# Splitting projection weights further ahead, on other engines, with extra transposes at the start of a two-layer hybrid encoder

## The chip, the cores and the metric

The kernel is one program on one core of a Trainium2 chip. The metric is the device time of one execution in microseconds. The kernel before was timed three times: 1618.01, 1619.09 and 1620.23 us, a median of 1619.09 us.

## The reference

The model is an encoder trunk of two layers over one sequence of 512 tokens and 1024 features. Each layer normalises its input, projects it with a matrix of 1024 x 4608, mixes over the sequence with two groups of heads, projects back, and adds a mixture of 16 experts, each of which picks 64 tokens.

```python
IN_WIDTHS = [RET_WIDTH] * 4 + [HGRN_WIDTH] * 5        # nine groups of 512 columns

def hybrid_mixer(xn, w_in, ret_g, hgrn_g, w_out, lb):
    proj = xn @ w_in
    rq, rk, rv, rg, hq, hf_fwd, hf_bwd, hi, hg = jnp.split(proj, splits, axis=-1)
    q, k = rotary(rq), rotary(rk) * RET_HEAD_DIM ** -0.5
    r_out = retention, forward and backward, of (q, k, rv), normalised, * silu(rg)
    q2, v2 = silu(hq) * HGRN_HEAD_DIM ** -0.5, hi
    f = lb + (1 - lb) * sigmoid(hf)                   # one per direction
    h_out = gated scan, forward and backward, of (q2, 1 - f, v2, log f), normalised, * silu(hg)
    return jnp.concatenate([r_out, h_out], axis=-1) @ w_out

h = x
for layer in range(2):
    h = h + hybrid_mixer(rms_norm(h, norm1_g[layer]), w_in[layer], ...)
    h = h + expert_choice_ffn(rms_norm(h, norm2_g[layer]), ...)
return rms_norm(h, final_norm_g)
```

Everything is float32.

## The kernel before

The instructions of every engine stand in the order in which the Python code issues them; the framework adds the semaphore waits. Each engine works through its own queue in order, so an instruction that waits holds up all that stand behind it on its engine.

**Start.** `start` (L364) loads nothing itself: the input rows come in four DMAs, one for each tile of 128 tokens. `turn_in` (L345) transposes blocks of 128 x 128 on TensorE into PSUM tiles `pb`, for the feature blocks 0 to 3 and one token tile after another. `stream` (L353) scales each feature block and splits it into a high part (ScalarE, L362) and a low part (VectorE, L363). `norm_gain` (L211) transposes one small tile of gains.

**Projections.** A float32 product is made of three products of rounded parts: high weight times high input, low weight times high input, high weight times low input. `proj` (L458) makes one group of 512 columns of the input projection: four quarters of 256 input features, each of 24 matmuls of 512 columns (L479). The nine groups are taken in the order `GROUPS`, counted here from 0 (`n`) or as first to ninth: silu query, the two forget gates (second and third), the value `v2` (fourth), then the rotary query and key, the retention value and gate, and the last gate.

**Splitting.** `split` (L437) makes the parts of the weights, one quarter at a time. The high part is a copy on ScalarE (L450), the low part a subtraction (L453) on VectorE, or on GpSimd for odd quarters of the groups 7 and 2, which are the fourth and the seventh in order. `proj` calls `split` at the start of each quarter with a number of quarters to be ahead: one in the first three groups and in the ninth, two in the others. Each split quarter occupies one of 22 slots of SBUF from its splitting until the last of its 24 matmuls; the raw half group that feeds two quarters occupies another one. Slots are handed out in order, and `pump` issues a weight load on SyncE's queue when a slot is free.

**Scans.** With the fourth group the scan over the first pair of the gated heads begins (`hgrn_pair`, L575). It is a generator that is advanced between blocks of six matmuls, with a budget for each group. Its first steps are, for both heads of the pair: the sum of the two keys on GpSimd (L604), the product of gates and query on VectorE (L605), two interleaved products (L615, L616), a high part on ScalarE (L618), a low part on VectorE (L621), then a product with a 0/1 matrix on TensorE (L629, four matmuls for each head). Six levels follow, each with products on VectorE (L587, L592), a product of decays on GpSimd (L597), a copy on ScalarE (L567) and score matmuls (L642). The second pair of heads goes through the same steps during the fifth and sixth group. In a layer the evacuation of a projection is on VectorE (L489) and ScalarE (L510, L511).

**Experts.** After the mixer come the output projection (L963), the routing and 16 experts in eight pairs, whose weights (192 MB in a layer) pass once through the same slots.

Of the kernel before, what the change touches and what calls it, by code (L numbers as in the profile page):

```python
# [16 lines left out]
P = 128  # L17
S = 512
D = 1024
NT = S // P  # L20
# [45 lines left out]
class Kernel:  # L66
# [298 lines left out]
    def start(self):  # L365

        self.begin(0)
        self.new_squares()
        for tt in range(NT - 1):
            self.squares(tt, 0, 0, 512, self.nc.scalar)  # L370
            self.squares(tt, 1, 512, 512, self.nc.vector)
        self.turn_in(range(4), range(2))
        self.norm_gain()
        self.turn_in(range(4), range(2, NT))
        self.stream(0)
        self.split(0)
        self.stream(1)
# [57 lines left out]
    def split(self, upto):  # L435


        nc = self.nc
        while self.nsplit <= min(upto, 4 * len(self.GROUPS) - 1):
            i = self.nsplit  # L440
            self.nsplit += 1
            g, j, jj = self.GROUPS[i // 4], i % 4 // 2, i % 2
            if jj == 0:
                self.raw = self.take(("in", self.mix_layer, g, j))
            part = self.slot([2, 2, 512], F32R)
            wh, low = part[:, 0], part[:, 1]
            src = self.raw.rearrange("p a k c -> p (a k) c")[:, 2 * jj:2 * jj + 2]
            e = nc.gpsimd if self.GROUPS[i // 4] in (7, 2) and i % 2 or i == 0 and self.mix_layer else nc.vector
            for ks in ((slice(0, 1), slice(1, 2)) if i == self.mix_layer == 0 else (slice(0, 2),)):
                nc.scalar.activation(wh[:, ks], src[:, ks], AF.Copy)  # L450
                if ks.start:
                    e = nc.gpsimd
                e.tensor_tensor(low[:, ks], src[:, ks], wh[:, ks], op=OP.subtract)  # L453
            self.parts[i] = part
            if jj:
                self.put(self.raw)

    def proj(self, n, natural, evacuate):  # L458


        nc = self.nc
        pg = [self.pj() for _ in range(4)]
        for q in range(4):
            self.split(4 * n + q + (2 if 2 < n < 8 else 1))
            part = self.parts.pop(4 * n + q)
            wh, low = part[:, 0], part[:, 1]

            if n == q == 0:
                order = [(c, k2, m) for k2 in range(2) for m in (0, 2, 1) for c in range(4)]
            elif n == 0 and q < 3:  # L470
                order = [(c, k2, m) for k2 in range(2) for c in range(4) for m in range(3)]
            else:
                order = [(c, k2, m) for c in range(4) for k2 in range(2) for m in range(3)]
            for i, (c, k2, m) in enumerate(order):
                cs = slice(c * P, (c + 1) * P)
                k = 2 * q + k2
                w, x = (wh, low, wh)[m][:, k2], (self.xH, self.xH, self.xL)[m][k // 4][:, k % 4]
                lhsT, rhs = (x[:, cs], w) if natural else (w[:, cs], x)
                nc.tensor.matmul(pg[c], lhsT=lhsT, rhs=rhs, start=(k == 0 and m == 0), stop=(k == ND - 1 and m == 2))  # L479
                if k == ND - 1 and m == 2:  # L480
                    evacuate(c, pg[c])
                if i == 23:
                    self.put(part)
                if i % 6 == 5:
                    yield
# [961 lines left out]
```

## Time and profile before

| what | value |
|---|---|
| median of three runs | 1619.09 us |
| the profiled execution | 1617.86 us |
| its span, first to last instruction | 1616.1 us |
| TensorE busy | 1537.6 us, 95% |
| VectorE, ScalarE, GpSimd busy | 671.3, 479.2, 207.8 us |
| matmuls of the input projection (L479) | 424.9 us, 1728 instructions |
| matmuls of the expert gates (L1208) | 476.7 us, 2048 instructions |
| read from HBM | 459.03 MB |

The profiled execution takes 1617.86 us, 1.76 us more than its span, since some time passes outside the first and last instruction. In the rows below, PE is TensorE, PEld its weight loads, DVE VectorE, ACT ScalarE, POOL GpSimd and SP SyncE. A row of a timeline merges neighbouring instructions of one line; the text in brackets is idle time of the engine before the row, with what ended it. In a table of stretches the column PEclk is the granted TensorE clock as a share of full speed. Layer 0 begins its fourth group at about 84 us, layer 1 at about 879 us.

### The profile page before, as it was taken

Reading aid. Unit: us, or ns where it says so; the run is one execution under the profiler, and the core shown is the slowest. Engines: PE = TensorE matmul, PEld = TensorE weight load, DVE = VectorE, ACT = ScalarE, POOL = GpSimd, SP = SyncE. Lnnn points to the kernel's source line nnn. Section 1 sums busy time; section 2 is a strip of 40 time slices with the busy share of each in tenths; the row PEclk is TensorE's granted clock in tenths of the full one; section 3 lists DMA queues with packets and bytes.
Section 4 is the critical chain, followed back from the end, with each engine's and each line's share of the span. In section 5 each row is a group of like instructions: output and inputs, shape, how many; then the busy total and the mean of one; then the engine's idle time right before and its main releaser. Section 6 shows DMA issues by size and latency. Waiting matters only on the chain. (4 is left out here: it accounts for less than half of the span.)

```text
span 1616.1 us, 20044 instructions
## 1 busy us (share of the span) xinstructions
PE 1537.6 (95%) x8020; PEld 957.6 (59%) x8020; DVE 671.3 (42%) x1132; ACT 479.2 (30%) x888; POOL 207.8 (13%) x197
## 2 busy tenths in 40 slices
PE   8999999989999999999999999999899999999986
PEld 6878787765354534533488787877545345444333
DVE  4488855661021312311255988375502123222113
ACT  4444444542221200200243444355313102112003
POOL 1043431100000000011001234320000000000201
PEclk9999999999999999999999999999999999999999
DMA  7211122679999999999960211217899999999997
GB/s 262 80 53 53 67 85 79 235 287 357 426 421 426 426 426 427 426 426 427 401 232 27 79 53 53 100 65 274 327 395 426 424 426 426 427 426 427 427 425 267
DMA packets 94605, 464.53 MB, mean 287 GB/s; under 512 B 7904, under 2 KB 16288, under 8 KB 48432
## 3 DMA queue, kind: packets, MB, share of 16 engines
q1 hardware_dynamic: 93040, 458.35, 69.9%
q0 software_dynamic: 1472, 4.90, 0.8%
q8 instruction: 63, 1.03, 0.2%
q14 instruction: 30, 0.25, 0.0%
HBM read 459.03 MB, written 4.19 MB: 287 GB/s over the span
## 5 line engine op out<-in xcount | busy, mean ns | idle before, releaser
L1208 PE MATMUL pj<-s,s 128*64 128x512 f32 x2048 | 476.7, 596 | 18.1 <-DMA s<-in_w_up_dram 14.6
L479 PE MATMUL pj<-s,s 128*128 128x512 f32 x1728 | 424.9, 400 | 3.5 <-DVE s L551 1.6
L479 PEld LDWEIGHTS pj<-s,s 128*128 128x128 f32 x1728 | 323.2, 191 | 70.8 <-DVE s L551 2.5
L1208 PEld LDWEIGHTS pj<-s,s 128*64 128x64 f32 x2048 | 172.2, 137 | 279.9 <-issue 206.9
L1352 PE MATMUL pb<-s,t 128*64 128x512 f32 x896 | 197.6, 594 | 5.6 <-ACT t L1246 2.7
L1352 PEld LDWEIGHTS pb<-s,t 128*64 128x64 f32 x896 | 64.0, 137 | 128.9 <-issue 115.0
L1256 DVE SCALAR_TENSOR_TENSOR t<-pb,sm,t 128x512 fp32r<-128x512 f32 (+1 forms) x34 | 24.4, 719 | 240.6 <-ACT t L1255 239.2
L1268 DVE TENSOR_TENSOR s<-s,pb 128x512 f32<-128x512 f32 (+1 forms) x112 | 67.3, 662 | 130.1 <-PE pb L1263 130.1
L1125 POOL TENSOR_TENSOR t<-s,t 128x512 fp32r<-128x512 f32 x16 | 20.9, 1330 | 696.8 <-ACT t L1123 696.8
L453 DVE TENSOR_TENSOR s<-s,s 128x1024 fp32r<-128x1024 f32 (+1 forms) x63 | 81.4, 1303 | 47.5 <-ACT s L450 47.3
L963 PE MATMUL pj<-s,s 128*128 128x512 f32 x384 | 95.1, 398 | 0.4 <-DVE t L489 0.4
L1173 DVE COPY sm<-pb 128x2 f32<-128x2 f32 x16 | 2.5, 159 | 203.2 <-PE pb L1170 203.2
L1255 ACT ACTIVATE t<-pb,sm 128x512 fp32r<-128x512 f32 (+1 forms) x34 | 22.5, 662 | 194.8 <-PE pb L1352 183.3
L963 PEld LDWEIGHTS pj<-s,s 128*128 128x128 f32 x384 | 69.9, 189 | 16.0 <-DVE t L489 1.3
L1184 ACT ACTIVATE t<-pb 128x512 fp32r<-128x512 f32 x16 | 9.6, 602 | 221.8 <-PE pb L1182 221.8
L450 ACT ACTIVATE s<-s 128x1024 fp32r<-128x1024 f32 (+1 forms) x73 | 74.1, 1035 | 0.1
L1151 PEld LDWEIGHTS pb<-t,t 128*128 128x128 f32 x512 | 65.7, 202 | 14.2 <-issue 9.7
L1151 PE MATMUL pb<-t,t 128*128 128x256 f32 x512 | 70.2, 295 | 2.1 <-DVE t L1135 1.3
L1263 PE MATMUL pb<-t,t 128*128 128x512 f32 (+1 forms) x256 | 66.7, 401 | 0.1
L1263 PEld LDWEIGHTS pb<-t,t 128*128 128x128 f32 x256 | 44.7, 188 | 33.1 <-issue 19.4
L1229 ACT ACTIVATE t<-pj,sm 128x512 f32<-128x512 f32 x32 | 22.0, 687 | 139.4 <-PE pj L1208 139.4
L567 ACT ACTIVATE s<-s 128x256 f32<-128x256 f32 x96 | 35.2, 415 | 80.1 <-DVE s L587 74.6
(235 smaller groups left out, 1587.2 us busy)
## 6 DMA issues: line engine op xcount, KB each, us to landing
s<-in_w_gate_dram SPq DMA_DIRECT2D x124, 1024.0 KB, 19.5
s<-in_w_up_dram SPq DMA_DIRECT2D x124, 1024.0 KB, 19.5
s<-in_w_down_dram SPq DMA_DIRECT2D x112, 1024.0 KB, 19.5
s<-in_w_in_dram SPq DMA_DIRECT2D x34, 1024.0 KB, 4.9
s<-in_w_down_dram SPq DMA_DIRECT2D x32, 512.0 KB, 10.4
s<-in_w_out_dram SPq DMA_DIRECT2D x8, 1024.0 KB, 4.8
s<-in_x_dram SPq DMA_DIRECT2D x8, 512.0 KB, 3.7
s<-in_w_gate_dram SPq DMA_DIRECT2D x8, 512.0 KB, 11.3
```

Of the source, the lines that this page charges most:

```text
L450: nc.scalar.activation(wh[:, ks], src[:, ks], AF.Copy)
L453: e.tensor_tensor(low[:, ks], src[:, ks], wh[:, ks], op=OP.subtract)
L479: nc.tensor.matmul(pg[c], lhsT=lhsT, rhs=rhs, start=(k == 0 and m == 0), stop=(k == ND - 1 and m == 2))
L567: self.nc.scalar.activation(kv[:, :, e], src, AF.Copy)
L963: nc.tensor.matmul(po[tt, f], lhsT=x, rhs=w, start=(k == 0 and i == 0), stop=(k == ND - 1 and i == 2))
L1151: nc.tensor.matmul(pt[:, i], lhsT=x[:, tt, k % 2::2], rhs=oh[:, tt], start=(tt == 0 and x is self.picked[u][0]), stop=(tt == NT - 1 and x ...
L1208: nc.tensor.matmul(pg[n + 2 * f][e * CAP:(e + 1) * CAP], lhsT=self.xe[:, k, at + e * CAP:at + (e + 1) * CAP], rhs=w[e][:, f * 512:(f + 1) ...
L1255: nc.scalar.activation(yH[0][:, cs], py, AF.Copy, scale=gate)
L1256: v.scalar_tensor_tensor(yL[0][:, cs], py, gate, yH[0][:, cs], op0=OP.mult, op1=OP.subtract)
L1263: nc.tensor.matmul(pc, lhsT=ohT[:, tt * P:(tt + 1) * P], rhs=y[:, cs], start=(y is yH[0]), stop=(y is yL[0]))
L1268: v.tensor_tensor(dst, dst, pc, op=OP.add)
L1352: nc.tensor.matmul(py[f][e * CAP:(e + 1) * CAP], lhsT=hT[:, k, e * CAP:(e + 1) * CAP], rhs=W[e][:, k2, f * 512:(f + 1) * 512], start=(k == ...
```

## The change

Three things are edited. At the start of layer 0, 16 transposes of the identity into a PSUM tile that nobody reads stand between the transposes of the input: five after the first token tile, and two, two and seven after the others. The odd quarters of the fourth group have their low part made on VectorE. The number of quarters that splitting is ahead comes from `lead_of`: in the first group one for the first two quarters and two for the last two (before: one), in the second group two (before: one), in the third group three and then four (before: one), and the rest as before.

```diff
-        self.turn_in(range(4), range(2))
-        self.norm_gain()
-        self.turn_in(range(4), range(2, NT))
+        unread = self.pj()
+        for tt, n in enumerate((5, 2, 2, 7)):
+            self.turn_in(range(4), [tt])
+            if tt == 1:
+                self.norm_gain()
+            for _ in range(n):
+                self.nc.tensor.transpose(unread[:, :P], self.ident, self.ident)
...
-            e = nc.gpsimd if self.GROUPS[i // 4] in (7, 2) and i % 2 or i == 0 and self.mix_layer else nc.vector
+            e = nc.gpsimd if self.GROUPS[i // 4] == 2 and i % 2 or i == 0 and self.mix_layer else nc.vector
...
+    @staticmethod
+    def lead_of(n, q):
+        if n == 2:
+            return 3 if q < 2 else 4
+        return 1 if n == 8 or n == 0 and q < 2 else 2
...
-            self.split(4 * n + q + (2 if 2 < n < 8 else 1))
+            self.split(4 * n + q + self.lead_of(n, q))
```

In the changed kernel the lines behind the first edit stand 5 lower, and those behind `lead_of` 12 lower: the low part L453 is L458, the evacuation L489 is L501, L604 is L616, L597 is L609, L605 is L617, L615 and L616 are L627 and L628, L621 is L633, L329 stays.

TensorE at the start of the program, from the last transpose of the first token tile on, before (`s_1` and `s_2` are the input, the four `pb` the PSUM tiles of its transposes, L214 the small transpose of the gains):

```order
L350 MATMUL pb_117<-ident,s_1_78 128x128
L350 MATMUL pb_114<-ident,s_1_78 128x128
L350 MATMUL pb_115<-ident,s_1_78 128x128
L350 MATMUL pb_116<-ident,s_1_78 128x128
L350 MATMUL pb_117<-ident,s_1_78 128x128
L214 MATMUL pj_126<-ident,t_3_83 128x16
L350 MATMUL pb_114<-ident,s_2_79 128x128
```

The same place now (`pj_114` is the unread tile):

```order
L350 MATMUL pb_118<-ident,s_1_78 128x128
L379 MATMUL pj_114<-ident 128x128 x5
L350 MATMUL pb_115<-ident,s_1_78 128x128
L350 MATMUL pb_116<-ident,s_1_78 128x128
L350 MATMUL pb_117<-ident,s_1_78 128x128
L350 MATMUL pb_118<-ident,s_1_78 128x128
L214 MATMUL pj_132<-ident,t_3_83 128x16
L379 MATMUL pj_114<-ident 128x128 x2
L350 MATMUL pb_115<-ident,s_2_79 128x128
```

The unread transposes stand in TensorE's own queue, so the transposes of the next token tile begin after them.

VectorE in the first group of layer 0, around the four short instructions that make the row norms (L329 to L332), before:

```order
L326 SCALAR_TENSOR_TENSOR sm_250<-sm_101 128x4
L453 TENSOR_TENSOR s_40_253<-s_6_99,s_40_253 128x1024
L329 RECIPROCAL sm_250<-sm_250 128x4
L330 TENSOR_TENSOR sm_250<-sm_250 128x4
L331 SCALAR_TENSOR_TENSOR sm_250<-sm_250 128x4
L332 SCALAR_TENSOR_TENSOR sm_249<-sm_250 128x4
L453 TENSOR_TENSOR s_46_299<-s_27_162,s_46_299 128x1024
```

The same place now:

```order
L326 SCALAR_TENSOR_TENSOR sm_267<-sm_101 128x4
L458 TENSOR_TENSOR s_41_270<-s_6_99,s_41_270 128x1024
L458 TENSOR_TENSOR s_42_273<-s_28_179,s_42_273 128x1024
L329 RECIPROCAL sm_267<-sm_267 128x4
L330 TENSOR_TENSOR sm_267<-sm_267 128x4
L331 SCALAR_TENSOR_TENSOR sm_267<-sm_267 128x4
L332 SCALAR_TENSOR_TENSOR sm_266<-sm_267 128x4
L458 TENSOR_TENSOR s_49_321<-s_28_179,s_49_321 128x1024
```

The low part of the second group's first quarter has moved ahead of the reciprocal, and the second quarter's low part stands where the first one stood.

VectorE from the third to the fourth group of layer 0, from the low parts of the third group's stretch to the first low part of the scan, before (`pj` rows are the evacuation of the third group):

```order
L453 TENSOR_TENSOR s_79_611<-s_70_494,s_79_611 128x1024
L489 TENSOR_TENSOR s_57_390<-pj_524,s_42_289 128x512
L489 TENSOR_TENSOR s_57_390<-pj_525,s_42_289 128x512
L489 TENSOR_TENSOR s_58_391<-pj_526,s_42_289 128x512
L489 TENSOR_TENSOR s_58_391<-pj_527,s_42_289 128x512
L453 TENSOR_TENSOR s_86_660<-s_77_564,s_86_660 128x1024
L605 TENSOR_TENSOR s_88_671<-s_57_390,s_47_308 128x1024 x2
L615 TENSOR_TENSOR s_89_672<-s_89_672,s_47_308 128x256x2
L616 TENSOR_TENSOR s_89_672<-s_59_392,s_88_671 128x256x2
```

The same place now:

```order
L458 TENSOR_TENSOR s_82_609<-s_71_484,s_82_609 128x1024
L458 TENSOR_TENSOR s_83_612<-s_79_560,s_83_612 128x1024
L458 TENSOR_TENSOR s_85_641<-s_79_560,s_85_641 128x1024
L501 TENSOR_TENSOR s_59_410<-pj_544,s_45_311 128x512
L501 TENSOR_TENSOR s_59_410<-pj_545,s_45_311 128x512
L501 TENSOR_TENSOR s_60_411<-pj_546,s_45_311 128x512
L501 TENSOR_TENSOR s_60_411<-pj_547,s_45_311 128x512
L617 TENSOR_TENSOR s_90_691<-s_59_410,s_50_330 128x1024 x2
L627 TENSOR_TENSOR s_91_692<-s_91_692,s_50_330 128x256x2
```

All four low parts of the fourth group now stand ahead of the evacuation of the third, and none is left between the evacuation and the first step of the scan.

GpSimd at the same place before, from the first low part of the fourth group on (`s_92_700` is the second one):

```order
L453 TENSOR_TENSOR s_85_657<-s_70_494,s_85_657 128x1024
L604 TENSOR_TENSOR s_89_672<-s_59_392 128x512
L604 TENSOR_TENSOR s_90_681<-s_59_392 128x512
L453 TENSOR_TENSOR s_92_700<-s_77_564,s_92_700 128x1024
L597 TENSOR_TENSOR s_89_672<-s_57_390 128x512
L597 TENSOR_TENSOR s_90_681<-s_57_390 128x512
```

The same place now:

```order
L616 TENSOR_TENSOR s_91_692<-s_61_412 128x512
L616 TENSOR_TENSOR s_92_701<-s_61_412 128x512
L609 TENSOR_TENSOR s_91_692<-s_59_410 128x512
L609 TENSOR_TENSOR s_92_701<-s_59_410 128x512
L609 TENSOR_TENSOR s_59_410<-s_91_692 128x2x128
```

Both low parts are gone from GpSimd, and its two decay products follow at once on the two sums of keys.

## Rows read from the trace of the kernel before

**Rows 1.** Who TensorE waited for: us in total, times, longest us

```profile
PE pj L1208 <- DMA s<-in_w_up_dram: 14.6, 13, 1.3
PE pb L629 <- DVE s L621: 6.4, 4, 2.1
...
PE pj L479 <- DVE s L453: 0.9, 1, 0.9
```

**Rows 2.** Timeline, TensorE, layer 0, groups two to four: start us, us, engine, line

```profile
45.07 53.35 PE L479 MATMUL pj<-s,s 128*128 128x512 f32 x233 [0.91 <-DVE s L453]
98.26 0.63 PE L629 MATMUL pb<-s,parity 128*128 128x512 f32 x2
...
107.47 3.00 PE L479 MATMUL pj<-s,s 128*128 128x512 f32 x12
```

**Rows 3.** The same, layer 0, second pair of heads

```profile
170.87 2.03 PE L629 MATMUL pb<-s,parity 128*128 128x512 f32 x8
...
174.98 3.00 PE L479 MATMUL pj<-s,s 128*128 128x512 f32 x12
```

**Rows 4.** The same, layer 1, fourth group

```profile
893.10 0.73 PE L629 MATMUL pb<-s,parity 128*128 128x512 f32 x2
...
902.85 3.00 PE L479 MATMUL pj<-s,s 128*128 128x512 f32 x12
```

**Rows 5.** Stretches: us, PE, PEld, DVE, ACT, POOL busy, PEclk, DMA share, GB/s

```profile
104.00:105.00 1.00, 1.00 (x4) 0.81 (x3) 1.00 (x2) 0.44 (x2) 1.00 (x1) 0.50 1.00 381
330.00:340.00 10.00, 10.00 (x62) 8.07 (x61) 8.17 (x29) 3.41 (x11) 0.00 (x0) 1.00 0.03 7
980.00:990.00 10.00, 7.87 (x34) 5.92 (x33) 9.22 (x13) 3.95 (x8) 3.55 (x4) 0.83 0.00 0
```

**Rows 6.** Timeline, VectorE, layer 0, third and fourth group

```profile
64.52 4.63 DVE L453 TENSOR_TENSOR s<-s,s 128x1024 fp32r<-128x1024 f32 x4 [1.18 <-ACT s L450]
79.19 0.69 DVE L489 TENSOR_TENSOR s<-pj,s 128x512 f32<-128x512 f32 x1 [10.04 <-PE pj L479]
...
83.27 0.69 DVE L489 TENSOR_TENSOR s<-pj,s 128x512 f32<-128x512 f32 x1 [0.67 <-PE pj L479]
87.23 2.58 DVE L453 TENSOR_TENSOR s<-s,s 128x1024 fp32r<-128x1024 f32 x1 [3.26 <-ACT s L450]
89.73 4.55 DVE L605 TENSOR_TENSOR s<-s,s 128x1024 f32<-128x1024 f32 x2
...
98.50 4.52 DVE L621 TENSOR_TENSOR s<-s,s 128x1024 fp32r<-128x1024 f32 x2
```

**Rows 7.** Timeline, GpSimd, the same stretch

```profile
88.68 4.51 POOL L604 TENSOR_TENSOR s<-s 128x512 f32<-128x512 f32 x2
98.67 3.27 POOL L453 TENSOR_TENSOR s<-s,s 128x1024 fp32r<-128x1024 f32 x1 [5.48 <-ACT s L450]
```

**Rows 8.** Timeline, VectorE, layer 1, third and fourth group

```profile
879.04 0.48 DVE L517 TENSOR_SCALAR s<-s,lbwork 128x512 f32<-128x512 f32 x1
...
884.44 2.31 DVE L605 TENSOR_TENSOR s<-s,s 128x1024 f32<-128x1024 f32 x1
...
893.88 4.53 DVE L621 TENSOR_TENSOR s<-s,s 128x1024 fp32r<-128x1024 f32 x2
```

**Rows 9.** Timeline, TensorE, the start of layer 0

```profile
7.08 1.12 PE L350 MATMUL pb<-ident,s 128*128 128x128 f32 x4 [1.64 <-DMA s<-in_x_dram]
...
11.61 7.12 PE L479 MATMUL pj<-s,s 128*128 128x512 f32 x24 [0.83 <-ACT s L450]
...
31.34 1.05 PE L418 MATMUL pb<-ident,sm 128*128 128x128 f32 x8
32.15 5.72 PE L479 MATMUL pj<-s,s 128*128 128x512 f32 x24
```

**Rows 10.** Timeline, weight loads of TensorE, the start

```profile
9.66 0.71 PEld L350 LDWEIGHTS pb<-ident,s 128*128 128x128 f32 x4 [0.53 <-DMA s<-in_x_dram]
```

**Rows 11.** Timeline, VectorE, the row norms of layer 0

```profile
29.19 0.16 DVE L332 SCALAR_TENSOR_TENSOR sm<-sm 128x4 f32<-128x4 f32 x1
```

## The prediction

> **What bounds the kernel.** I read first who TensorE waits for [rows 1]. TensorE is nearly always busy, so the reader looks for the waits that are left in the mixers: two large ones are named there, L629 for VectorE's low part L621 (6.4 us in 4 waits) and L479 for VectorE's low part L453 (0.9 us). The timeline of TensorE puts them in place: one L479 wait of 0.91 us at 45.07 us, and the L629 waits at the beginning of the scan of the first pair of heads in both layers [rows 2, 4]. What such a place costs is more than its idle time. In the second pair the same run of instructions (8 of L629, 6 of L479, 8 of L642) takes from 170.87 to 174.98 us, 4.11 us [rows 3]; in the first pair of layer 0 it takes from 98.26 to 107.47, 9.21 us [rows 2], and in layer 1 from 893.10 to 902.85, 9.75 us [rows 4]. The excess is 5.10 and 5.64 us. The stretches show why it goes beyond the idle time: after the waits the granted clock is 0.50, the level of 1.2 GHz [rows 5].
>
> Then I read VectorE's timeline backwards from L621 [rows 6]. Its chain begins with L605 at 89.73 and ends with the second L621 at 98.50 + 4.52 = 103.02, 13.29 us later. L605 itself could have begun after the last evacuation, at 83.27 + 0.69 = 83.96, but the low part of a quarter of the fourth group stands in front of it: 3.26 us of waiting for ScalarE's copy, then 2.58 us. In layer 1 the chain runs from 884.44 to 893.88 + 4.53 = 898.41, 13.97 us, while the last work on the third group's gates ends at 879.04 + 0.48 = 879.52 [rows 8].
>
> **The change part by part.** Durations are of the profiled execution, 1617.86 us with a span of 1616.1; it stands 1.23 us under the median of the runs, so the sum is made as a difference and taken from the median.
>
> *The lead of the third group, and VectorE for the fourth group's odd quarters.* These go together. No low part is left between the evacuation and L605. If the chain takes as long as before, it ends at 83.96 + 13.29 = 97.25 in layer 0 and at 879.52 + 13.97 = 893.49 in layer 1. TensorE comes to the first head's L629 at 98.26 and 893.10, and to the second head's four matmuls later; at the pace of the row of eight (2.03 us with its tail, so about 0.9 us for four) that is 99.2 and 894.0 [rows 2 to 4]. The second L621 is what the second head needs, so it is there 1.9 and 0.5 us early. The first L621 ends half of that row sooner, by 2.2 us, and is early too. The chain should even be shorter: GpSimd's low part of 3.27 us lies beside the two L621 [rows 7], which take 2.26 us each against 1.16 us for one of the four L453 of the same size at 64.52 [rows 6]. Against that stands that the two L597 now follow the two L604 and lie beside the chain; they have the shape of L604, whose two take 4.51 us beside VectorE [rows 7], 1.24 us more than the 3.27 that leaves. With all of that added, layer 0 still waits for nothing and layer 1 waits 0.7 us. I take the whole excess: 5.10 + 5.64 = 10.74 us, with 9.5 as the lower end for this reason.
>
> The three low parts that are moved cost VectorE about 3 x 1.16 us and ScalarE as much in the third group, where VectorE is idle for 10.04 us before the evacuation at 79.19 [rows 6]: nothing. If that cover were gone, the evacuation would come later and with it L605, which has 1.9 us of room in layer 0.
>
> *The lead of the second group, and of the second half of the first.* The wait of 0.91 us at 45.07 is for the second low part of the second group, split after a run of short instructions on VectorE. It now stands a quarter earlier. The whole 0.91 us goes. In exchange one more low part stands ahead of the reciprocal of the row norms, 1.16 us, with its copy on ScalarE. The last step L332 ends at 29.19 + 0.16 = 29.35 [rows 11]; TensorE needs it at 31.34 [rows 9]. So the norms have about 2.0 us of room, and 1.16 us fits: nothing. (Both move together when TensorE is earlier, since the norms follow from its transposes.) Queued behind that reciprocal are only the evacuations of the first group.
>
> *The unread transposes.* The five after the first token tile fall into TensorE's wait of 1.64 us for the second tile [rows 9]. At 0.18 us each (0.71 us for four weight loads, [rows 10]) they take 0.9 us: free. The next four take 0.72 us, of which 0.53 us was a wait for the fourth tile [rows 10]; so the fourth tile's transposes come 0.19 us later, and ScalarE's chain to the first matmul with them. The last seven take 1.3 us and end about when that chain ends: free. What they can bring is pace. The first 24 matmuls of the projection take 7.12 us, the same 24 at 32.15 us take 5.72 us [rows 9], although the table of stretches shows a granted clock of 1.00 for both. Matmuls that start slow and speed up after TensorE has been busy for a while look like the lower clock, and TensorE will now be busy from 7.08 on. I take the full 1.40 - 0.19 = 1.2 us; the ends are -0.2 us (no effect) and 2 us (some transposes are faster too).
>
> Here a rule speaks against the change. The Trainium skill, "TensorE: Matmul & The Clock Gate", Part 4: PE-mode transpose, states that work in transpose mode does not release the clock gate as matmuls do. No row of this trace can decide it, since no stretch holds transposes alone for long. By that rule this part would be worth -0.2 us; it is a rival below.
>
> *The sum:* 10.74 + 0.91 + 1.2 = 12.85 us less. In what follows, the experts' weights are loaded into slots that TensorE frees, and just before that stream begins the DMA share is 0.03 while TensorE is fully busy [rows 5]: the stream begins with TensorE's progress, so the gain is passed on. 1619.09 - 12.85 = 1606.2 us.
>
> **Rivals.**
>
> *The transposes do not raise the clock.* For it: only the pace of matmuls speaks for the other reading, and late operands would slow the first 24 as well. Against it: the wait before them is the only one that is shown. Price: 1.40 us; time 1607.6.
>
> *VectorE becomes the bound, and the wait moves to the second pair of heads.* For it: VectorE is busy 9.22 us of 10 at 980 us, where TensorE is idle for 2 us [rows 5]. In the fourth group VectorE itself loses only one low part, 2.58 us; if it sets the pace from there on, that is all that remains in each layer: 10.74 - 2 x 2.58 = 5.6 us come back. Time 1611.8. Against it: at the second pair's L629 TensorE waits for nothing [rows 3], so VectorE has caught up by then.
>
> *The experts absorb it.* TensorE waits 14.6 us there for w_up [rows 1]. If their stream ended when it did, all of the mixers' gain would be gone: 1619.1. Against it stands the idle queue just before the stream.
>
> *Slower: the slots.* The longer lead holds up to three more slots while the third and fourth group run, and the loads wait for slots. Where a half group lands too late, its split is late on ScalarE, TensorE stands for up to a quarter, 5.72 us, and afterwards runs slow: at 980 us the granted clock is 0.83 on average, so 0.17 x 10 x 2 = 3.4 us at half speed, 1.7 us lost [rows 5]. If this befalls the fourth and the fifth group of both layers, it costs 4 x 7.4 = 29.7 us: 1635.9. It decides once a load comes later than its split; at 64.52 four splits run one behind the other, with 1.18 us of waiting, and that for ScalarE [rows 6].
>
> **Chances.** The forecast 0.48, the clock not raised 0.30, VectorE the bound 0.13, the experts absorb it 0.05, slower by the slots 0.04. The forecast's time is the likeliest: 1606.2 us. For the range: two stretches at the lower clock could vanish or appear elsewhere as everything shifts, 1.7 us each, so the low end is 1606.2 - 3.4 - 0.8 = 1602; the high end takes in the second rival, 1612. A difference under 0.2%, 3.2 us, can't be told from none in this kernel. The first three cases are all faster by more than that: 0.91. The fourth is the same, with a little of the third: 0.05. Slower: 0.04.
>
> **What would show it.** In the profile after, the list of TensorE's waits has no L629 on L621 (now L641 on L633) and no L479 wait on the low part; from the first of the L629 matmuls to the projection's matmuls behind the first eight score matmuls about 4.1 us pass in both layers, and the clock is 1.00 there. The first 24 matmuls take about 5.7 us if the transposes raise the clock, 7.1 us if not. Room for error shows as a wait at the row norms' product L418, at the second pair's L642 or L479, or at the split copies on ScalarE for a load. The forecast is wrong if those new waits add up to more than 6 us, or if the first expert matmul does not come about 7 us earlier.

## The result and the profile after

The changed kernel took 1603.16 us, the median of four runs (1601.83 to 1604.05). The kernel before, run beside it, took 1618.55 us. The ratio is 0.9907 with a 95% interval of 0.9895 to 0.9919: 15.4 us or 0.93% less, and the whole interval lies beyond the 0.2% under which the prediction called a difference none. The forecast was 1606.2 us in a range of 1602 to 1612. The time lies in the range; the forecast gain of 12.85 us lies just under the interval of the measured one, 13.1 to 17.0 us.

The profiled execution took 1603.25 us with a span of 1601.5, against 1617.86 and 1616.1 before. So the rows have to account for 14.6 us. Line numbers are 5 or 12 higher than before.

The list of TensorE's waits after (us in total, times, longest):

```profile
PE pj L1220 <- DMA s<-in_w_up_dram: 14.4, 13, 1.4
PE pb L654 <- ACT s L579: 5.9, 4, 1.7
...
PE pj L491 <- DVE s L563: 1.6, 2, 0.8
```

The 6.4 us of L629 for L621 and the 0.9 us of L479 for L453 [rows 1] have no successor. What is now second is L654 for the copy L579; the same wait, L642 for L567, was 2.4 us before. TensorE's timeline in layer 0 shows the place of the scan's first pair:

```profile
36.80 58.78 PE L491 MATMUL pj<-s,s 128*128 128x512 f32 x258
95.42 2.03 PE L641 MATMUL pb<-s,parity 128*128 128x512 f32 x8
...
99.53 3.00 PE L491 MATMUL pj<-s,s 128*128 128x512 f32 x12
```

The wait at 45.07 is gone: one row of 258 matmuls runs to the scan. From the first L641 to the matmuls behind the first score matmuls 4.11 us pass instead of 9.21 [rows 2]. Layer 1 reads the same, 4.11 us instead of 9.75 [rows 4]:

```profile
885.19 2.03 PE L641 MATMUL pb<-s,parity 128*128 128x512 f32 x8
...
889.30 3.00 PE L491 MATMUL pj<-s,s 128*128 128x512 f32 x12
```

Why TensorE no longer waits is seen on VectorE, layer 0 [rows 6]:

```profile
61.89 6.90 DVE L458 TENSOR_TENSOR s<-s,s 128x1024 fp32r<-128x1024 f32 x6 [1.18 <-ACT s L455]
76.57 0.69 DVE L501 TENSOR_TENSOR s<-pj,s 128x512 f32<-128x512 f32 x1 [7.77 <-PE pj L491]
...
80.65 0.69 DVE L501 TENSOR_TENSOR s<-pj,s 128x512 f32<-128x512 f32 x1 [0.67 <-PE pj L491]
81.26 3.47 DVE L617 TENSOR_TENSOR s<-s,s 128x1024 f32<-128x1024 f32 x2
...
88.91 2.51 DVE L633 TENSOR_TENSOR s<-s,s 128x1024 fp32r<-128x1024 f32 x2
```

Six low parts lie ahead of the evacuation, in time in which VectorE had nothing to do, and it still idles for 7.77 us. L617 follows the evacuation at once, and the chain takes 10.16 us (81.26 to 91.42) instead of 13.29. It ends 4.0 us before TensorE comes. In layer 1 it ends at 885.11, 0.1 us before TensorE's row begins and about 1 us before the second head's part of it:

```profile
874.35 2.06 DVE L617 TENSOR_TENSOR s<-s,s 128x1024 f32<-128x1024 f32 x1
...
882.58 2.53 DVE L633 TENSOR_TENSOR s<-s,s 128x1024 fp32r<-128x1024 f32 x2
```

The start of the program on TensorE [rows 9]:

```profile
5.16 1.27 PE L379 MATMUL pj<-ident 128*128 128x128 f32 x5
6.84 1.11 PE L350 MATMUL pb<-ident,s 128*128 128x128 f32 x4 [0.41 <-DMA s<-in_x_dram]
...
10.72 0.94 PE L379 MATMUL pj<-ident 128*128 128x128 f32 x7
11.58 5.75 PE L491 MATMUL pj<-s,s 128*128 128x512 f32 x24
```

The first 24 matmuls take 5.75 us instead of 7.12. They begin at full pace, and already the seven transposes ahead of them take 0.13 us each where the first five took 0.25.

### The profile page after: what moved, and what is told of

The parts are those of the page before. It is cut to its first block, busy times and chain, and to the rows that moved or that the text cites. A ratio compares the mean times of both kernels' runs of the same rounds, so it can differ in the third digit from the quotient of the medians.

```text
span 1601.5 us, 20071 instructions
## 1 busy us (share of the span) xinstructions
PE 1531.0 (96%) x8036; PEld 958.7 (60%) x8036; DVE 665.3 (42%) x1136; ACT 479.5 (30%) x888; POOL 191.8 (12%) x193
## 5 line engine op out<-in xcount | busy, mean ns | idle before, releaser
L491 PE MATMUL pj<-s,s 128*128 128x512 f32 x1728 | 417.0, 394 | 1.6 <-DVE s L563 1.6
L491 PEld LDWEIGHTS pj<-s,s 128*128 128x128 f32 x1728 | 318.2, 188 | 65.8 <-DVE s L563 2.4
L458 DVE TENSOR_TENSOR s<-s,s 128x1024 fp32r<-128x1024 f32 (+1 forms) x67 | 82.5, 1250 | 39.5 <-ACT s L455 39.2
L975 PE MATMUL pj<-s,s 128*128 128x512 f32 x384 | 95.2, 398 | 0.4 <-DVE t L501 0.4
L975 PEld LDWEIGHTS pj<-s,s 128*128 128x128 f32 x384 | 69.9, 189 | 16.0 <-DVE t L501 1.2
L579 ACT ACTIVATE s<-s 128x256 f32<-128x256 f32 x96 | 35.2, 415 | 76.6 <-DVE s L599 70.8
```

The costliest lines, as they stand in the source:

```text
L579: self.nc.scalar.activation(kv[:, :, e], src, AF.Copy)
L975: nc.tensor.matmul(po[tt, f], lhsT=x, rhs=w, start=(k == 0 and i == 0), stop=(k == ND - 1 and i == 2))
```

## The experiments

Each ratio is to the kernel before on the same chip in the same minutes. The sharper measure is a stretch of TensorE's timeline between two instructions that every kernel has: where nothing stalls it repeats within 0.05 us from one kernel to another. In the table, N is the start of the row norms' product (L418 before), P1 and P2 the start of the L629 matmuls of the first and the second pair, and E the start of the transposes of the second pair's keys (L657 before). All in us. "Start" is N counted from the beginning of the span.

| run | median | ratio to before, 95% interval | start | N-P1 | P1-P2 | P2-E | layer 1: N-P1 | P1-P2 | P2-E |
|---|---|---|---|---|---|---|---|---|---|
| before | 1618.55 | | 31.34 | 66.92 | 72.61 | 47.51 | 65.49 | 73.13 | 47.54 |
| after | 1603.16 | 0.9907 (0.9895-0.9919) | 29.95 | 65.47 | 67.51 | 47.48 | 64.86 | 67.49 | 47.50 |
| transposes alone | 1616.21 | 0.9986 (0.9978-0.9995) | 29.65 | 66.90 | 72.81 | 47.48 | 65.51 | 73.13 | 47.54 |
| third group's lead alone | 1605.65 | 0.9921 (0.9908-0.9933) | 31.47 | 66.70 | 67.51 | 47.48 | 64.86 | 67.51 | 47.48 |
| VectorE alone | 1614.11 | 0.9971 (0.9960-0.9982) | 31.77 | 66.73 | 69.30 | 47.50 | 65.56 | 72.73 | 47.50 |
| early lead alone | 1617.95 | 0.9994 (0.9985-1.0003) | 32.20 | 65.65 | 72.47 | 47.50 | 65.50 | 73.18 | 47.50 |
| after, GpSimd back | 1603.72 | 0.9908 (0.9894-0.9921) | 30.64 | 65.47 | 67.51 | 47.48 | 64.86 | 67.51 | 47.49 |
| after, lead of two | 1609.19 | 0.9941 (0.9928-0.9953) | 31.38 | 65.47 | 68.18 | 47.49 | 64.86 | 72.22 | 47.50 |
| after, short lead | 1605.01 | 0.9916 (0.9902-0.9929) | 30.88 | 65.47 | 67.51 | 48.96 | 64.86 | 67.51 | 48.16 |
| after, all on VectorE | 1602.61 | 0.9901 (0.9888-0.9915) | 30.33 | 65.47 | 67.51 | 46.96 | 64.86 | 67.51 | 46.95 |
| after, seven transposes | 1601.92 | 0.9903 (0.9889-0.9916) | 31.13 | 65.47 | 67.51 | 47.50 | 64.86 | 67.51 | 47.46 |
| after, matmuls | 1603.05 | 0.9906 (0.9893-0.9920) | 29.69 | 65.47 | 67.51 | 47.46 | 64.86 | 67.51 | 47.49 |
| all on VectorE, lead 3, 3 | 1603.58 | 0.9910 (0.9897-0.9924) | 29.47 | 65.47 | 67.51 | 46.92 | 64.86 | 67.51 | 46.92 |
| all on VectorE, lead 4, 3 | 1606.09 | 0.9924 (0.9911-0.9936) | 29.64 | 65.47 | 67.51 | 48.29 | 64.86 | 67.51 | 48.32 |

The experts' part, counted from the routing (L1099 before) to the next N or, in layer 1, to the last products (L1339), varies from run to run, 465.9 to 468.5 us in layer 0 and 447.4 to 449.2 in layer 1, in no order that follows the mixers. That is why a median tells less.

**The unread transposes alone.**

```diff
+        unread = self.pj()
+        for tt, n in enumerate((5, 2, 2, 7)):
+            self.turn_in(range(4), [tt])
+            if tt == 1:
+                self.norm_gain()
+            for _ in range(n):
+                self.nc.tensor.transpose(unread[:, :P], self.ident, self.ident)
```

> The kernel before with the 16 unread transposes alone. Theory (the parts add, and the transposes raise the clock): the first 24 matmuls of the projection take about 5.7 us instead of 7.1, and the time is about 1.4 us under the kernel before. Rival (transposes do not raise the clock; the first 24 became faster because something else in the changed kernel came earlier): the 24 still take 7.1 us and the time is 0 to 0.2 us longer.

The first 24 matmuls took 5.74 us, N came 1.69 us earlier, and the runs give 2.2 us less (0.8 to 3.6). The theory holds, the rival falls.

**The lead of the third group alone**, GpSimd still making the odd low parts of the fourth.

```diff
+    def lead_of(n, q):
+        if n == 2:
+            return 3 if q < 2 else 4
+        return 2 if 2 < n < 8 else 1
...
-            self.split(4 * n + q + (2 if 2 < n < 8 else 1))
+            self.split(4 * n + q + self.lead_of(n, q))
```

> The kernel before with the lead of the third group alone (three, three, four, four quarters); GpSimd still makes the odd low parts of the fourth group, now about two quarters sooner. Theory: the lead is what matters, since it takes the low part from between the evacuation and the first step of the scan; GpSimd's second low part may hold up its sum of two keys by up to 3.3 us, for which there is room of some 4 us. The waits at the two L629 go, 9 to 10.7 us less than before. Rival (VectorE for the odd quarters is needed too, since GpSimd's work beside VectorE stretches the chain): a wait of about 1 us stays in each layer with the lower clock behind it, 4 to 7 us less.

12.8 us less, more than expected. The stretches P1-P2 are those of the changed kernel and give 10.7 us of it, N-P1 another 0.85. GpSimd's and VectorE's timelines (L454 is the low part, L612 the sum of keys, L629 the scan's low part):

```profile
68.50 6.38 POOL L454 TENSOR_TENSOR s<-s,s 128x1024 fp32r<-128x1024 f32 x2 [26.53 <-ACT s L451]
80.76 2.71 POOL L612 TENSOR_TENSOR s<-s 128x512 f32<-128x512 f32 x2 [5.89 <-ACT s L518]
```

```profile
91.74 2.58 DVE L629 TENSOR_TENSOR s<-s,s 128x1024 fp32r<-128x1024 f32 x2
```

GpSimd had finished at 74.88 and was idle for 5.89 us before its sums. The chain ended at 94.32; TensorE came at 98.17. The rival falls: VectorE is not needed for the odd quarters.

**VectorE for the odd quarters of the fourth group alone.**

```diff
-            e = nc.gpsimd if self.GROUPS[i // 4] in (7, 2) and i % 2 or i == 0 and self.mix_layer else nc.vector
+            e = nc.gpsimd if self.GROUPS[i // 4] == 2 and i % 2 or i == 0 and self.mix_layer else nc.vector
```

> The kernel before with VectorE for the odd quarters of the fourth group alone, and no longer lead. Two or three low parts then stand on VectorE between the evacuation of the third group and the first step of the scan, 1.2 us each, and no GpSimd low part lies beside the two low parts of the scan (2.5 us for both instead of 4.5). Theory (lead and engine are worth something each, and both remove VectorE time from one chain): the chain of the scan ends 1 to 4 us sooner, the time is 3 to 9 us less. Rival (without the lead nothing is won, what is saved on L621 is spent on the added low parts): within 2 us of the kernel before.

4.3 us less, of it 3.3 in P1-P2 of layer 0 and 0.4 in that of layer 1. VectorE and TensorE in layer 1 (L454 the low part, L629 the scan's low part, L637 the product):

```profile
887.29 1.22 DVE L454 TENSOR_TENSOR s<-s,s 128x1024 fp32r<-128x1024 f32 x1 [2.13 <-ACT s L451]
...
890.51 2.57 DVE L629 TENSOR_TENSOR s<-s,s 128x1024 fp32r<-128x1024 f32 x2
```

```profile
891.78 1.20 PE L637 MATMUL pb<-s,parity 128*128 128x512 f32 x4 [2.96 <-DVE s L629]
```

A low part between two steps of the chain costs its 1.2 us and the 2.13 us in which VectorE waits, in order, for ScalarE's copy. The layers differ in what is left at L637: in layer 0 a wait of 1.09 us with the clock at 1.00 behind it, in layer 1 one of 2.96 us with the clock at 0.50 between 893.6 and 896.6. Together with the run before, where GpSimd made these low parts and the wait went, this shows that the place mattered and not the engine.

**The lead of the first two groups alone.**

```diff
+    def lead_of(n, q):
+        if n == 2:
+            return 1
+        return 1 if n == 8 or n == 0 and q < 2 else 2
...
-            self.split(4 * n + q + (2 if 2 < n < 8 else 1))
+            self.split(4 * n + q + self.lead_of(n, q))
```

> The kernel before with the lead of the first and second group alone. Theory: the wait of 0.91 us at 45 us goes and the time is 1.0 to 2.1 us less (in the changed kernel the stretch between 38 and 98 us is 1.45 us shorter, and layer 1 has brought another 0.6 us before its fourth group). Rival (what the changed kernel gained there belongs to the clock or to the lead of the third group): no difference within 0.4 us.

N-P1 in layer 0 is 1.27 us shorter, as the theory has it, but layer 1 gains nothing (65.50): the 0.63 us there come with the third group's lead, as the run with that lead alone shows (64.86). By the runs the difference, 0.5 us, is not told from none.

**The changed kernel with GpSimd back for the fourth group.**

```diff
-            e = nc.gpsimd if self.GROUPS[i // 4] == 2 and i % 2 or i == 0 and self.mix_layer else nc.vector
+            e = nc.gpsimd if self.GROUPS[i // 4] in (7, 2) and i % 2 or i == 0 and self.mix_layer else nc.vector
```

> The changed kernel, but GpSimd makes the odd low parts of the fourth group as before. Theory (the lead does it all): with the lead of the third group alone GpSimd made both low parts by 75 us, before its sum of the keys at 81 us, so nothing lies beside the chain any more; the time is that of the changed kernel within 1 us, about 15.4 us under the kernel before, and the chain of the scan ends some 4 us ahead of TensorE in layer 0. Rival (the VectorE edit adds its share, as in the run with it alone, which was 4.3 us faster than before): 3 to 4 us slower than the changed kernel, about 12 us under the kernel before.

1603.72 us, and every stretch of the table behind N agrees with the changed kernel within 0.02 us. One of the change's parts does nothing once the lead is there.

**A lead of two in the third group.**

```diff
         if n == 2:
-            return 3 if q < 2 else 4
+            return 2
```

> The changed kernel with a lead of two quarters all through the third group, so that two low parts of the fourth group come after the evacuation again, both on VectorE, 1.2 us each, the second possibly with 2.1 us of waiting for ScalarE's copy. In the changed kernel the chain ends 4.9 us before the second head needs it in layer 0 and 1.0 us in layer 1. Theory (what counts is whether the chain is late at L641, by this room): nothing lost in layer 0, in layer 1 a wait of 1.4 to 3.5 us at L641 and one stretch at half speed, 1.7 us more: 2 to 5 us slower than the changed kernel, 10 to 13 us under the kernel before. Rival (two quarters are enough, the third and fourth only hold slots): within 1 us of the changed kernel.

By the ratios 0.34% slower than the changed kernel, 5.5 us, a little over the theory's 5: 0.7 us in layer 0, where it had expected nothing, and 4.7 in layer 1. In layer 0 both low parts came with a wait for ScalarE's copy (2.31 and 2.13 us), and the chain ended at 98.75; the last two L641 waited for it until 98.81. VectorE and TensorE in layer 1:

```profile
884.02 1.23 DVE L458 TENSOR_TENSOR s<-s,s 128x1024 fp32r<-128x1024 f32 x1 [2.13 <-ACT s L455]
```

```profile
888.51 1.19 PE L641 MATMUL pb<-s,parity 128*128 128x512 f32 x4 [2.47 <-DVE s L633]
```

The wait is in the range of the theory, what follows it cost more: 2.47 and 0.16 us of waiting made 4.7 us, and for 3.4 us behind them the granted clock was 0.50, the level of 1.2 GHz. The room in the chain is the right quantity, and two quarters do not give it.

**A shorter lead for the seventh group**, to unload the second pair's stretch.

```diff
+        if n == 5 or n == 6 and q == 0:
+            return 1
```

> The changed kernel with a shorter lead for the seventh group: one quarter in the sixth group and in the first quarter of the seventh, so that two low parts less, one of them GpSimd's of 2.4 us, lie in the second pair's stretch at 165 to 185 us, where TensorE waits 1.2, 0.8 and 1.7 us. Theory (VectorE sets the pace of that stretch, 9 to 10 of 10 us busy): these waits shrink, 2 to 6 us less than the changed kernel over both layers. Rival (the stretch is set by the order of copies and products of the scan, or the parts are now late for the seventh group): no difference within 1 us, or up to 4 us slower with new waits of the projection for a low part.

The waits of the scan shrank from 5.9 to 3.0 us, as the theory said, but the rival won. GpSimd and TensorE (L493 is the projection):

```profile
181.32 2.81 POOL L458 TENSOR_TENSOR s<-s,s 128x1024 fp32r<-128x1024 f32 x1
```

```profile
184.18 1.42 PE L493 MATMUL pj<-s,s 128*128 128x512 f32 x5 [1.50 <-POOL s L458]
```

GpSimd's low part was ready at 184.13, and TensorE had already come for it. P2-E grew by 1.5 and 0.7 us. The two layers run alike up to the score matmuls behind this wait; there the granted clock was 0.50 between 186 and 189 us in layer 0 and 1.00 in layer 1, and the same eight matmuls that take 1.13 us in layer 1 take 2.04:

```profile
186.44 2.04 PE L656 MATMUL pb<-s,s 128*128 128x128 f32 x8 [0.83 <-ACT s L581]
```

About 1.3 us are lost there in layer 0, against 0.5 us at a later wait in layer 1: here the lower clock was not free.

**No low parts on GpSimd.**

```diff
-            e = nc.gpsimd if self.GROUPS[i // 4] == 2 and i % 2 or i == 0 and self.mix_layer else nc.vector
+            e = nc.gpsimd if i == 0 and self.mix_layer else nc.vector
```

> The changed kernel with VectorE for the odd low parts of the seventh group too, so that GpSimd makes no low part but the first one of layer 1. Theory (GpSimd beside VectorE costs VectorE more than the work it takes over: its low part at 166.64 us stretched an L571 from 0.7 to 1.2 and an L599 from 0.7 to 1.8 us, the one at 188.16 an L599 to 2.25, and it delays GpSimd's own product L564): VectorE gains 2 to 3 us of pace per low part for 1.2 us of work, 1 to 3 us less than the changed kernel over both layers. Rival (VectorE is the bound of the second pair's stretch and gets 1.2 us more work there in each layer): TensorE's waits for the scan grow by about 1.2 us in each layer, 1 to 3 us slower than the changed kernel.

P2-E fell by 0.52 and 0.55 us: VectorE, 10.00 of 10 us busy between 180 and 190 in the changed kernel, got 1.2 us more work per low part and became quicker. In the changed kernel the second of GpSimd's low parts ran from 188.16 to 190.98, and the first had pushed GpSimd's own product L564 to 168.99. VectorE beside these two, then the same instructions in this run:

```profile
169.50 1.77 DVE L599 TENSOR_TENSOR s<-s,s 128x512 f32<-128x512 f32 x1
...
189.28 2.25 DVE L599 TENSOR_TENSOR s<-s,s 128x512 f32<-128x512 f32 x1
```

```profile
169.99 1.10 DVE L599 TENSOR_TENSOR s<-s,s 128x512 f32<-128x512 f32 x1
...
189.12 0.68 DVE L599 TENSOR_TENSOR s<-s,s 128x512 f32<-128x512 f32 x1
```

An L571, which the expectation names as stretched to 1.2 us, takes 1.27 in this run as well, so that part of the theory falls. Its direction is shown by the stretches; the ratio, 0.0006 lower with an interval of 0.0013 to either side, does not separate the two kernels.

**Only the last seven transposes.**

```diff
-        for tt, n in enumerate((5, 2, 2, 7)):
+        for tt, n in enumerate((0, 0, 0, 7)):
```

> The changed kernel with the last seven unread transposes only. In all runs with the sixteen, the first 24 matmuls of the projection took 5.5 to 5.8 us and the clock rose between 10.3 and 13.3 us; in those without, it rose between 14.6 and 17.1 us. Theory (TensorE has to be busy without a gap for some time before the clock rises, so the early ones count): with seven alone the clock rises after the first matmuls, at 13 to 15 us, and about half of the gain at the start is lost, 0.5 to 1 us slower than the changed kernel. Rival (only the gap just before the first matmul counts): the first 24 take 5.75 us as in the changed kernel, and the time is the same or 0.2 us better.

TensorE's timeline:

```profile
10.18 1.70 PE L379 MATMUL pj<-ident 128*128 128x128 f32 x7
11.53 6.75 PE L491 MATMUL pj<-s,s 128*128 128x512 f32 x23
```

The seven take 0.24 us each, the slow pace, and the first matmuls stay slow: up to 14.2 us they start 0.43 us apart, behind it 0.23. N comes at 31.13, 1.2 us later than in the changed kernel. So the early ones count. That TensorE must be busy without a gap is not shown: the changed kernel has a gap of 0.41 us before its second token tile and was fast before its first matmul. The ratio (0.9903) does not show it: 1.2 us is below what it can tell.

**Matmuls in place of the transposes.**

```diff
-                self.nc.tensor.transpose(unread[:, :P], self.ident, self.ident)
+                self.nc.tensor.matmul(unread[:, :P], lhsT=self.ident, rhs=self.ident, start=True, stop=True)
```

> The changed kernel with the 16 unread transposes written as ordinary matmuls of the identity by the identity, of the same 128 x 128 size. Theory (for the clock a transpose counts like a matmul): the clock rises at the same time as in the changed kernel, 10.3 to 13.3 us, the first 24 matmuls take 5.5 to 5.8 us, and the time is the same within 1 us. Rival (transposes count less): the clock rises clearly earlier than in the changed kernel, before 9 us, and the transposes of the input behind it go faster, 0.5 to 1 us less.

```profile
5.26 2.21 PE L379 MATMUL pj<-ident 128*128 128x128 f32 x10
7.30 0.60 PE L350 MATMUL pb<-ident,s 128*128 128x128 f32 x4
...
11.35 5.72 PE L491 MATMUL pj<-s,s 128*128 128x512 f32 x24
```

The rival is right on the clock: the input's transposes at 7.30 take 0.60 us for four instead of 1.11. It is wrong on the time: the first matmul begins at 11.35, no sooner than elsewhere (10.97 to 12.84), N comes at 29.69, and the median is the same. What differs is not only the mode. A matmul here is two instructions (ten for five), so the five fill 2.21 us instead of 1.27 and leave no gap before the second token tile, where the changed kernel has 0.41 us.

**All on VectorE, with a lead of three in the last two quarters of the sixth group.**

```diff
+        if n == 5 and q > 1:
+            return 3
```

> The run with VectorE for all odd low parts, with a lead of three quarters in the last two quarters of the sixth group. This moves one low part from 182.3 us, just ahead of the product L599 for which TensorE waits 1.71 us in each layer, to a place before the second pair's evacuations. Theory (VectorE sets the pace there, and a low part just ahead of L599 is on the chain): that wait shrinks by 1.2 to 1.4 us in each layer, and the time is 2 to 3 us under the run with VectorE for all, 18 to 19 us under the kernel before. Rival (the work only moves forward in the same chain): the waits before it grow by as much, and the time is the same within 1 us.

This edit stands beside that of the run without GpSimd's low parts. VectorE and TensorE (lines behind `lead_of` are 2 higher again, L656 is the score product):

```profile
182.58 0.89 DVE L601 TENSOR_TENSOR s<-s,s 128x512 f32<-128x512 f32 x1
```

```profile
178.79 1.16 PE L656 MATMUL pb<-s,s 128*128 128x128 f32 x8 [1.20 <-ACT s L581]
...
184.33 1.16 PE L656 MATMUL pb<-s,s 128*128 128x128 f32 x8 [0.55 <-ACT s L581]
```

The aimed-at wait fell from 1.71 to 0.55 us, and P2-E from 46.96 to 46.92: the rival. The one ahead grew from 0.79 to 1.20, and twelve matmuls ahead of that one took 3.44 us instead of 2.98.

**The same with four, then three.**

```diff
+        if n == 5 and q > 1:
+            return 6 - q
```

> As the last one, but with four quarters of lead in the third quarter of the sixth group, so that two low parts are moved ahead of the first products of the second pair's scan and none is left between these and the end of the evacuation. Theory: the three waits of 0.8, 0.8 and 1.7 us in each layer shrink to 1 us in all, and a new one of about 0.6 us appears at the first score matmuls, whose keys come 1.2 to 2.4 us later: 3 to 5 us under the run with VectorE for all, 19 to 21 us under the kernel before. Rival (the low parts, or the loads of their weights, are late there): a wait at the first score matmuls of 2 us or more in each layer, and nothing won against the last one.

```profile
167.58 1.23 PE L656 MATMUL pb<-s,s 128*128 128x128 f32 x8 [1.57 <-ACT s L581]
```

A new wait of 1.57 us at the first score matmuls instead of the 0.6 expected, and none of the later ones shorter than in the run before: P2-E is 1.4 us longer than there in both layers. No version measured here beats the changed kernel by more than a median can tell.

## Why the prediction was right

**The lead of the third group, with VectorE for the fourth.** 5.10 + 5.64 = 10.74 us were taken off; P1-P2 fell by 5.10 and 5.64. The reference for it, the same instructions at the second pair, was the right one, since the place now takes 4.11 us, as that one did [rows 3]. The step took both edits together, and there the runs correct it: the lead alone gives all of it, VectorE alone a third. What the prediction feared for layer 1, the two L597 beside the chain, did not come: in layer 0 L616 took 2.65 us and L609 3.04 for two, where L604 had taken 4.51 [rows 7], and L617 beside them 3.47 instead of 4.55; in layer 1 L609 took 2.41 us and ended at 875.33, when the chain had just begun. One reading was wrong without a consequence: the gate work of the third group does not end at 879.52 in layer 1 of the kernel before, since a last L516 and L517 run at 886.66, inside the chain whose 13.97 us the prediction took whole.

**The lead of the first two groups.** Its term, 0.91 us, was mis-sized: N-P1 fell by 1.45 us, of which 1.27 belongs to this lead. A further 0.2 in layer 0 and 0.63 in layer 1 come with the third group's lead and were in no term. Where they sat is seen by setting TensorE's matmuls before and after beside each other, one by one. At 45.07 us 1.19 us are lost, 0.91 of them shown as idle. In layer 0 about 0.2 us more is lost at 88.78, where TensorE came for the low part that GpSimd finished at 86.33 + 2.40 = 88.73; the timeline shows no wait there. In layer 1 it is 0.43 us at 883.48, 0.15 of them shown, again for GpSimd's low part, and 0.21 at the first L629. Before:

```profile
86.33 2.40 POOL L453 TENSOR_TENSOR s<-s,s 128x1024 fp32r<-128x1024 f32 x1 [44.63 <-ACT s L450]
```

So an idle time in the timeline was here a lower bound of what its removal gave.

**The unread transposes.** 1.2 us, measured 1.39 at N. The mechanism, a faster pace sooner, is shown: in the four runs without them the stretch from the first matmul to N took 19.73 to 21.17 us, in the eight with all sixteen transposes 18.36 to 18.54. What it is worth in one execution varies with the arrival of the input, since the first matmul began between 10.97 and 12.84 us. Averaged over these runs N came at 31.70 without and 30.24 with them, 1.46 us. The two terms inside the 1.2 are not right one by one. From the first matmul to N the runs with the transposes were 2.07 us shorter on average, not 1.40: the kernel before, from which the 1.40 was read, is the run without them that became fast earliest (its first 24 matmuls took 7.12 us, those of the other three 7.59 to 8.54). And their first matmul began 0.62 us later (11.84 against 11.22), not 0.19; how much of that is the transposes and how much the arrival of the input is not shown. That the difference came so near is in part luck. The first five took 1.27 us, not 0.9, and still fitted into the wait for the second token tile.

The rule of the Trainium skill against this part ("TensorE: Matmul & The Clock Gate", Part 4: PE-mode transpose), that transposes do not engage the full clock as matmuls do, is not borne out in that form. In the run "all on VectorE, lead 3, 3", when TensorE had done nothing but transposes, four of them went at the fast pace before the first matmul at 11.09:

```profile
9.10 0.66 PE L350 MATMUL pb<-ident,s 128*128 128x128 f32 x4
...
11.09 5.75 PE L493 MATMUL pj<-s,s 128*128 128x512 f32 x24 [0.58 <-ACT s L455]
```

In seven of the eight runs with all sixteen the pace rose before the first matmul; in the run with a lead of two it rose just behind it. That matmuls in their place brought the fast pace by 7.30 us is in the rule's direction. The gap is not the reason: in the run "all on VectorE, lead 4, 3" the transposes follow one another without a gap as the matmuls do, and they were still slow at 9.37:

```profile
6.41 1.06 PE L350 MATMUL pb<-ident,s 128*128 128x128 f32 x4
...
9.37 1.06 PE L350 MATMUL pb<-ident,s 128*128 128x128 f32 x4
```

This is one execution of each, and since a matmul is two instructions here, the mode and the number of instructions are not separated.

**The experts pass it on.** Their parts took 0.89 us more and 0.96 less than before, within their own spread, and the first expert matmul came 7.71 us earlier in layer 0 and 13.44 in layer 1. Right.

**VectorE as the new bound.** The rival was right about the place and wrong about the price. In the second pair's stretch of before the granted clock fell to 0.50 twice, for 3.4 us at 189 and at 984 us; in the changed kernel it did not. TensorE in the changed kernel:

```profile
178.69 1.16 PE L654 MATMUL pb<-s,s 128*128 128x128 f32 x8 [1.22 <-ACT s L579]
180.63 3.01 PE L491 MATMUL pj<-s,s 128*128 128x512 f32 x12 [0.79 <-DVE s L563]
185.37 1.16 PE L654 MATMUL pb<-s,s 128*128 128x128 f32 x8 [1.73 <-ACT s L579]
```

Before, the twelve matmuls that take 3.01 us here took 4.60 with the lower clock in them, and the eight behind them came without a wait:

```profile
188.57 4.60 PE L479 MATMUL pj<-s,s 128*128 128x512 f32 x12 [0.79 <-DVE s L551]
193.31 1.16 PE L642 MATMUL pb<-s,s 128*128 128x128 f32 x8
```

The time of the slower clock came back as a longer wait, and P2-E stayed at 47.5 us in both layers. VectorE has no idle time where that wait lies (the row from 180 to 190 us), and P2-E became shorter only in runs without GpSimd's low parts, where VectorE's products became quicker. So VectorE sets the pace there, as far as these runs show:

```profile
170.00:180.00 10.00, 8.63 (x49) 6.94 (x47) 8.89 (x11) 5.13 (x11) 5.81 (x6) 1.00 0.31 107
180.00:190.00 10.00, 7.64 (x41) 6.31 (x41) 10.00 (x14) 4.05 (x8) 4.66 (x4) 1.00 0.00 0
```

But this was so before the change, too, so nothing was given back; the rival took a limit of this stretch for a limit on what an earlier stretch can gain.

**The slots.** No load came later than its split: ScalarE's only waits for a DMA are the three for the input, 4.6 us against 4.8 before.

**The sum.** 12.85 us were forecast, 14.57 appear between the two timelines: 0.19 more from the transposes, 0.54 and 0.63 from N-P1, and 0.36 from the rest. The medians differ by 15.4 us, 0.8 more than the two profiled executions; single runs of one kernel spread over 2 us and more.

## What to carry to other kernels

Where an in-order engine carries both a chain that someone waits for and work that could be done earlier, place that work ahead of the chain, in the engine's idle time; which engine did it made no difference here once the place was right, and a step put between two others costs its own wait as well. Price such a stall by the same instructions at a place where they do not stall, not by the idle time shown. A faster clock or a shorter single wait is worth little in a stretch that another engine paces, and the run with the shorter lead shows that this must hold in the kernel at hand: measure the stretch between two fixed instructions.

## What the runs showed of the hardware

- GpSimd's low part of 128 x 1024 takes 2.4 to 3.3 us where VectorE's takes 1.2, and it slows VectorE while it runs: an L599 of 0.68 us took 2.25 beside it. Giving the work back to the busy engine shortened that stretch by 0.5 us in each layer.
- Transposes alone brought TensorE to its faster pace, the seven ahead of the first matmul taking 0.13 instead of 0.25 us each, and fewer of them did not (0.24 us).
- Where VectorE set the pace, the two levels of the clock did not show in P2-E: 47.51 us with 3.4 us at 1.2 GHz in it, 47.48 without. The run with the seven transposes has both in one execution: the clock was 0.50 from 182 to 184.5 us in layer 0 and 1.00 all through P2-E in layer 1, and P2-E was 47.50 and 47.46. With the shorter lead, where TensorE had waited for GpSimd's low part, the lower clock in layer 0 came with a P2-E of 48.96 us, against 48.16 in layer 1.
